# A two-layer attention encoder: its first loads, its x transposes and its bias lines in another order

## The chip, the cores and the metric

The kernel runs on one core of one Trainium2 chip. The metric is the device time of one execution in microseconds (us), as the median of three runs. The profile is one execution taken by the hardware profiler; it has a span (first to last instruction) and a device time of its own.

## The reference, cut to what matters

An input `x` of 512 tokens by 1024 features goes through two layers. Each layer normalises x, projects it with a packed weight matrix, runs four attention branches (A to D) with a gate each, merges them and adds the result to x:

```
for l in range(2):
    h = _rmsnorm(x, norm_gain[l])
    p = _project(h, w_in[l])                       # 1024 -> 13824 columns
    oa = _window_sink_attention(rms(a_q), rms(a_k), a_v, bias_a, sink[l])
    ob = _diff_attention(rms(b_q), rms(b_k), b_v, tbl_b, lam, ...)
    oc = _dense_gqa(rope(c_q), rope(c_k), c_v)
    od = _dilated_attention(rms(d_q), rms(d_k), d_v, bias_d)    # three groups
    for n, o in enumerate((oa, ob, oc, od)):
        y = (o * silu(p['gate'][n])) @ w_branch[l, n]
        merged = merged + sigmoid(p['merge'][n]) * y
    x = x + merged @ w_out[l]
```

`bias_a`, `tbl_b` and `bias_d` come from one small table `rel_bias` (32 buckets by 36 heads), looked up by the distance between query and key. For each head the bias is therefore one line over distances, of which every query sees a shifted piece.

## The kernel before, in words

**Work and tiles.** x is cut into four tiles of 128 tokens (tt = 0 to 3). A tile is normalised (`norm_a`: sum of squares on ACT, scaling on DVE into `h`), transposed, and split into a high and a low f16 part, `hT_h` and `hT_l`, which stay on the chip for the layer. In layer 0, tiles 0 to 2 are transposed on TensorE with the f32 identity (`norm_b`, 8 transposes a tile, then ACT and DVE split them); tile 3 is split first and then transposed by two DMA transposes from SP (`norm_t`, line 247). A projection (`proj_n`, lines 396 to 398) is, for each tile and each of 8 slices of k, three matmuls: high by high, high by low, low by high. For 512 columns that is 24 matmuls a tile.

**Weights.** Weights come in f32 pieces of 1 MB, as two tiles `wst` of 128x1024 each (line 125), with three buffers for such tiles. ACT makes the high part `whi` (line 142), DVE the low part `wlo` (line 143). `take_w` converts three pieces ahead (`AHEAD`) and issues the load of a fourth.

**Bias lines.** `bias_lines` splits `rel_bias` into three f16 parts on DVE (lines 262 to 268), multiplies it with a one-hot table `oh` of 97 rows by 2432 (7 matmuls of 8 output rows, line 274), and writes the result to the first 8 partitions of `acc` (lines 276 and 278). Line 929 then writes these 8 rows 23 times to the DRAM tensor `lines`. `load_bias` (line 542) reads shifted pieces of `lines` as the bias of a head; the first such reader is branch A.

**Order.** The first projections are q of branch A (`proj_q`), then k and v of A (`proj_kv`, 256 columns), then the gate of A beside the attention of A. Each engine runs its instructions in the order in which the program was laid out, so an instruction that waits holds up everything behind it on that engine. This order comes from a scheduler with a timeline of its own; `tc.issue_after(x)` tells it not to place a block ahead of x. SP's queue carries x, the weights, the DMA transposes (`hT`, `qs`, `kk`), `oh`, `lines` and the bias reads; POOL's queue carries the small tables (`gb`, `rope_t`, `sc`, `rbb`, `sk`, `lv`).

**Names in rows.** `mm` is a projection's PSUM tile, `p` that of the bias lines, `s` that of scores, `tr` that of transposes, `pv` that of probabilities by values. `t` is the score with its bias.

Of the kernel before, what the change touches and what calls it, by code (L numbers as in the profile page):

```python
# [11 lines left out]
F32 = mybir.dt.float32  # L12
# [9 lines left out]
HD = 64  # L22
# [65 lines left out]
AHEAD = 3  # L88


@with_exitstack
def encoder(ctx, tc, x, wf, norm_gain, qk_gain, sink, lambda_vec, sub_gain, rel_bias, onehot, rope, out):
# [83 lines left out]
    def load_x(src, tt):  # L176
        if tt % 2 == 0:
            x_sb[tt // 2] = qk.tile([128, 2, D], F32, tag="qx", name="xt", bufs=2)
        nc.sync.dma_start(out=x_sb[tt // 2][:, tt % 2, :], in_=src[tt * 128:tt * 128 + 128, :])
# [23 lines left out]
    with tc.issue_after(dma_w(1).ins):  # L203
        load_x(x, 2)
        nc.sync.dma_start(out=rb, in_=bass.AP(tensor=rel_bias.tensor, offset=rel_bias.offset, ap=[[0, 3], [36, 32], [1, 36]]))
        nc.sync.dma_start(out=oh, in_=onehot)
        load_x(x, 3)

    def norm_a(l, tt):

        xt = x_sb[tt // 2][:, tt % 2, :]
        ss = sm.tile([128, 2], F32, tag="n_ss", name="ss")
        for j in range(2):
            sq = tmp.tile([128, 512], F32, tag="sq", name="sq")
# [5 lines left out]
        S.activation(rs, ln, AF.Exp, scale=-0.5)  # L220
        hs = []
        for j in range(2):
            f = slice(512 * j, 512 * j + 512)
            h = tmp.tile([128, 512], F32, tag="gs", name="h", bufs=4)
            V.scalar_tensor_tensor(h, xt[:, f], rs, gain_b[l][:, f], op0=ALUm, op1=ALUm)
            hs.append(h)
        return hs

    def norm_b(tt, hs):

        for j in range(2):
            tr = transpose4(hs[j])
            d = slice(4 * j, 4 * j + 4)
            c = slice(tt * 128, tt * 128 + 128)
            S.activation(hT_h[:, d, c], tr, AF.Copy, scale=SH)
            done = V.scalar_tensor_tensor(hT_l[:, d, c], tr, SH, hT_h[:, d, c], op0=ALUm, op1=ALUs)
        return done

    def norm_t(tt, hs):

        hi = tmp.tile([128, 2, 512], F16, tag="st", name="h_hi", bufs=3)
        lo = tmp.tile([128, 2, 512], F16, tag="st", name="h_lo", bufs=3)
# [17 lines left out]
    def bias_lines():  # L260
# [7 lines left out]
        V.tensor_tensor(rb16[64:96, :], rb[64:96, :], rb16[64:96, :], op=ALUs)  # L268
        for i, (s0, ln_, h0, nh, off, w) in enumerate(SEG.values()):
            for e in range(0, ln_, 512):  # L270
# [173 lines left out]
    def proj_q(res, l, kind, col, perm=False):  # L444
# [4 lines left out]
        for tt in range(NT):  # L449
# [9 lines left out]
            st = tmp.tile([128, 4, 4, HD], F16, tag="st", name="st", bufs=3)  # L459
# [10 lines left out]
    def proj_k(res, l, kind, col, perm=False):  # L470
# [6 lines left out]
        for tt in range(NT):  # L477
# [33 lines left out]
    def proj_kv(res, l, kind, col):  # L511
# [6 lines left out]
        for tt in range(NT):  # L518
# [7 lines left out]
            st = tmp.tile([128, 4, 128], F16, tag="st", name="st", bufs=3)  # L526
# [59 lines left out]
    def gated(n, ft, gd):  # L586
# [3 lines left out]
        st = tmp.tile([128, 2, 512], F16, tag="st", name="st", bufs=3)  # L590
# [324 lines left out]
    for l in range(L):  # L915
# [109 lines left out]
```

## Time and profile before

| | us |
|---|---|
| median of 3 runs (1674.24 to 1674.72) | 1674.26 |
| device time of the profiled execution | 1674.46 |
| its span | 1672.4 |
| PE busy in it | 1602.6 (96%) |
| DVE busy | 1075.9 (64%) |
| ACT busy | 961.0 (57%) |
| POOL busy | 8.8 (1%) |

PE is busy throughout except at the start: of 40 slices of 41.8 us each, the first shows 3 tenths and the second 3. A busy PE need not be a full one, since matmuls overlap; the granted clock (PEclk) says at which rate it ran. The chain of waits and the waits by engine tell what ended each stretch in which PE stood still. In those two views an engine name with a q (SPq) is the engine's instruction queue, where a DMA is issued.

### The profile page before, as it was taken

The numbers are of one execution on the slowest core, as the hardware profiler recorded it, in microseconds if no ns is written. First come the engines' busy times: TensorE is split into PE (matmuls) and PEld (weight loads), VectorE is DVE, ScalarE is ACT, GpSimd is POOL, SyncE is SP. The second block draws the span as 40 slices with busy tenths as digits, with TensorE's granted clock in tenths as the row PEclk, the third lists the DMA queues.
The fourth block names the chain that finished last, engine by engine and source line by source line (L and its number), as shares of the span: only waits on it lengthen the run. The fifth ranks groups of instructions, "written<-read, shape, count | busy, mean of one in ns | idle before, by whom it ended". The sixth has DMA issues, their size and how long they took to land.

```text
span 1672.4 us, 26438 instructions
## 1 busy us (share of the span) xinstructions
PE 1602.6 (96%) x10302; PEld 834.6 (50%) x10302; DVE 1075.9 (64%) x2104; ACT 961.0 (57%) x1771; POOL 8.8 (1%) x32
## 2 busy tenths in 40 slices
PE   3389999999999999999999999999999999999999
PEld 1155545564555554454445554556455555445444
DVE  3368866785576766575556887678457676657451
ACT  3157676566664656564545767556667464556450
POOL 1000000000000000000000000000000000000000
PEclk8699999999999999999999999999999999999999
DMA  5974733352356757435357483336235674753421
GB/s 188 97 161 133 164 109 95 100 133 76 110 121 155 183 144 191 141 114 143 109 169 173 105 183 119 93 101 133 76 98 130 152 180 132 200 146 94 133 88 51
DMA packets 230817, 218.37 MB, mean 131 GB/s; under 512 B 176316, under 2 KB 188620, under 8 KB 230509
## 3 DMA queue, kind: packets, MB, share of 16 engines
q1 hardware_dynamic: 229925, 214.26, 50.0%
q0 software_dynamic: 768, 2.43, 0.5%
q8 instruction: 80, 1.31, 0.3%
q14 instruction: 44, 0.36, 0.1%
HBM read 163.94 MB, written 10.24 MB: 104 GB/s over the span
## 4 chain that ended last, share of the span: by engine, by line
PE 89%; DMA 6%; DVE 3%; ACT 1%; issue 0%; SPq 0%; DVEq 0%; ACTq 0%
PE mm L396 15%; PE mm L397 15%; PE mm L398 15%; PE mm L407 10%; PE mm L409 10%; PE mm L408 10%; PE s L560 3%; PE s L561 3%; PE pv L565 3%; DMA hT_h<-h_hi 2%; PE pv L567 2%; PE pv L566 2%; DMA oh<-in_onehot_dram 1%; DMA wst<-in_wf_dram 1%; DMA qs<-st 1%; DVE wlo L143 1%
## 5 line engine op out<-in xcount | busy, mean ns | idle before, releaser
L396 PE MATMUL mm<-whi,hT_h 128*128 128x512 f16 (+1 forms) x1408 | 522.7, 371 | 38.7 <-DMA hT_h<-h_hi 31.1
L397 PE MATMUL mm<-wlo,hT_h 128*128 128x512 f16 (+1 forms) x1408 | 522.6, 371 | 0.7 <-DVE wlo L143 0.7
L398 PE MATMUL mm<-whi,hT_l 128*128 128x512 f16 (+1 forms) x1408 | 522.2, 371 | 1.2 <-DMA hT_l<-h_lo 1.2
L143 DVE SCALAR_TENSOR_TENSOR wlo<-wst,whi 128x1024 f16<-128x1024 f32 (+1 forms) x260 | 307.3, 1204 | 203.1 <-ACT whi L142 202.0
L142 ACT ACTIVATE whi<-wst 128x1024 f16<-128x1024 f32 (+1 forms) x260 | 262.6, 1036 | 269.4 <-PE mm L408 122.3
L396 PEld LDWEIGHTS <-hT_h 128*128 128x128 f16 x1408 | 144.4, 103 | 175.9 <-DMA hT_h<-h_hi 32.1
L398 PEld LDWEIGHTS <-hT_l 128*128 128x128 f16 x1408 | 144.4, 103 | 147.6 <-issue 2.6
L397 PEld LDWEIGHTS <-hT_h 128*128 128x128 f16 x1408 | 144.4, 103 | 146.4 <-issue 7.7
L407 PE MATMUL mm<-hT_h,whi 128*128 128x512 f16 x512 | 194.1, 379 | 0.0
L409 PE MATMUL mm<-hT_h,wlo 128*128 128x512 f16 x512 | 194.1, 379 | 0.0
L408 PE MATMUL mm<-hT_l,whi 128*128 128x512 f16 x512 | 194.0, 379 | 0.0
L551 ACT ACTIVATE t<-t,nm 128x512 f32<-128x512 f32 (+2 forms) x224 | 132.0, 599 | 69.1 <-DVE t L811 24.1
L556 DVE TENSOR_TENSOR pl<-t,ph 128x512 f16<-128x512 f32 (+2 forms) x224 | 119.1, 543 | 37.8 <-ACT ph L555 36.5
L565 PE MATMUL pv<-v,ph 128*128 128x65 f16 (+2 forms) x992 | 123.8, 202 | 0.1
L566 PE MATMUL pv<-v,ph 128*128 128x64 f16 (+2 forms) x992 | 122.9, 201 | 0.0
L567 PE MATMUL pv<-v,pl 128*128 128x65 f16 (+2 forms) x992 | 121.0, 199 | 0.0
L409 PEld LDWEIGHTS <-wlo 128*128 128x128 f16 x768 | 75.1, 98 | 88.9
L407 PEld LDWEIGHTS <-whi 128*128 128x128 f16 x768 | 75.1, 98 | 87.1
L408 PEld LDWEIGHTS <-whi 128*128 128x128 f16 x768 | 75.1, 98 | 86.6
L555 ACT ACTIVATE ph<-t 128x512 f16<-128x512 f32 (+2 forms) x224 | 110.9, 506 | 2.8 <-PE pv L567 0.7
L560 PE MATMUL s<-qs,kk 128*128 128x512 f16 (+4 forms) x384 | 99.4, 293 | 1.7 <-DVE gs L582 1.3
L561 PE MATMUL s<-qs,kk 128*128 128x512 f16 (+4 forms) x384 | 100.5, 292 | 0.0
(173 smaller groups left out, 1925.4 us busy)
## 6 DMA issues: line engine op xcount, KB each, us to landing
wst<-in_wf_dram SPq DMA_DIRECT2D x264, 512.0 KB
dsc<-num SPq DMA_DIRECT2D x16, 260.0 KB
xt<-in_x_dram SPq DMA_DIRECT2D x8, 512.0 KB
bias_b<-lines SPq DMA_DIRECT2D x8, 448.0 KB
bias_a<-lines SPq DMA_DIRECT2D x16, 192.0 KB
num<-dsc SPq DMA_DIRECT2D x8, 260.0 KB
n<-dsc SPq DMA_DIRECT2D x8, 260.0 KB
bias_d<-lines SPq DMA_DIRECT2D x32, 64.0 KB
```

The costliest lines, as they stand in the source:

```text
L142: S.activation(hi[:, a], st[:, e:e + step], AF.Copy if sc is SW else AF.Identity, scale=sc)
L143: V.scalar_tensor_tensor(lo[:, a], st[:, e:e + step], sc, hi[:, a], op0=ALUm, op1=ALUs)
L396: PE.matmul(p[:, :ncol], a, wh, start=(k == 0), stop=False)
L397: PE.matmul(p[:, :ncol], a, wl, start=False, stop=False)
L398: PE.matmul(p[:, :ncol], b, wh, start=False, stop=(k == 7))
L407: PE.matmul(p, wh[:, k, f], rh[:, k], start=(k == 0), stop=False)
L408: PE.matmul(p, wh[:, k, f], rl[:, k], start=False, stop=False)
L409: PE.matmul(p, wl[:, k, f], rh[:, k], start=False, stop=(k == nk - 1))
L561: PE.matmul(p, klo, q, start=False, stop=True)
L565: PE.matmul(o, ph, vt[:, 0:d + 1], start=start, stop=False)
L566: PE.matmul(o[:, 0:d], ph, vt[:, d + 2:2 * d + 2], start=False, stop=False)
L567: PE.matmul(o, pl, vt[:, 0:d + 1], start=False, stop=stop)
```

## The change

Six things are altered.

1. Loads. On SP the order of the first loads is x tile 0, gain, weight piece 0, x tile 1, weight piece 1, x tiles 2 and 3, then weights. `rb` and `oh` leave SP for POOL's queue. All tables on POOL now stand behind a one-element copy (`there`) that waits for the last x tile.
2. Weight staging has five buffers (`WST`) instead of three; the conversions of pieces 0 and 1 are placed by `issue_after`.
3. Tile 3 of layer 0 is transposed on TensorE like the others (layer 1 keeps its DMA transposes).
4. `bias_lines` multiplies with `rbr`, in which the 8 heads are repeated 16 times, so that `acc` has the 8 lines on all 128 partitions (16 copies). `lines` is written by two DMAs from POOL, of 128 and of 56 partitions. The call stands behind the k and v projection instead of ahead of it.
5. In `proj_k` the tile `st` of 16x128 is two tiles of 8x128, with a copy and a DMA transpose each; there are four buffers of that tag instead of three.
6. `load_x`, `norm_b` and the block for tables return or use handles for `issue_after`.

```diff
+WST = 5
...
-            st = wp.tile([128, 1024], F32, tag="wst", name="wst", bufs=3)
+            st = wp.tile([128, 1024], F32, tag="wst", name="wst", bufs=WST)
...
     with tc.issue_after(dma_w(1).ins):
         load_x(x, 2)
-        nc.sync.dma_start(out=rb, in_=bass.AP(tensor=rel_bias.tensor, offset=rel_bias.offset, ap=[[0, 3], [36, 32], [1, 36]]))
-        nc.sync.dma_start(out=oh, in_=onehot)
-        load_x(x, 3)
+        last_x = load_x(x, 3)
+
+    there = const.tile([128, 1], F32, name="there")
+    tables = G.tensor_copy(there, x_sb[1][:, 1, 0:1])
...
+        rbr = const.tile([97, len(SEG), 128], F16, name="rbr")
         for i, (s0, ln_, h0, nh, off, w) in enumerate(SEG.values()):
+            V.tensor_copy(rbr[:, i].rearrange("p (c h) -> p c h", h=8),
+                          rb16[:, h0:h0 + 8].unsqueeze(1).to_broadcast([97, 16, 8]))
...
-                PE.matmul(p[:8, :n], rb16[:, h0:h0 + 8], oh[:, c], start=True, stop=True)
+                PE.matmul(p[:, :n], rbr[:, i], oh[:, c], start=True, stop=True)
...
+        for c0, c1_ in ((0, 16), (16, COPIES)):
+            nc.gpsimd.dma_start(out=lines[c0:c1_].rearrange("c h n -> (c h) n"), in_=accf[0:8 * (c1_ - c0), 0:LINE])

     for tt in range(NT):
-        normed = (norm_b if tt < 3 else norm_t)(tt, norm_a(0, tt))
-        if tt < 2:
-            load_w(tt)
+        normed, split = norm_b(tt, norm_a(0, tt))
+        if tt == 0:
+            with tc.issue_after(scaled[0].ins):
+                load_w(0)
+            with tc.issue_after(split.ins):
+                load_w(1)
...
-            st = tmp.tile([128, 16, 128], F16, tag="st", name="st", bufs=3)
-            hi = st[:, 0:8, 0:HD]
+            st = [tmp.tile([128, 8, 128], F16, tag="st", name="st", bufs=4) for _ in range(2)]
+            hi = st[0][:, :, 0:HD]
...
-            V.tensor_copy(st[:, :, HD:128], st[:, :, 0:HD])
-            nc.sync.dma_start_transpose(out=kk[:, :, tt * 128:tt * 128 + 128], in_=st.rearrange("p a d -> p (a d)"))
+            for i in range(2):
+                V.tensor_copy(st[i][:, :, HD:128], st[i][:, :, 0:HD])
+                nc.sync.dma_start_transpose(out=kk[:, 8 * i:8 * i + 8, tt * 128:tt * 128 + 128],
+                                            in_=st[i].rearrange("p a d -> p (a d)"))
...
-            bias_lines()
-            with tc.issue_after(normed.ins):
+            with tc.issue_after(normed.ins), tc.issue_after(tables.ins):
                 gain_tables(0)
+                nc.gpsimd.dma_start(out=rb, in_=bass.AP(tensor=rel_bias.tensor, offset=rel_bias.offset,
+                                                        ap=[[0, 3], [36, 32], [1, 36]]))
+                nc.gpsimd.dma_start(out=oh, in_=onehot)
         run(qa, proj_kv(r, l, "A", 512))
         if l == 0:
-            nc.sync.dma_start(out=lines.rearrange("c h n -> h c n"),
-                              in_=accf[0:8, 0:LINE].unsqueeze(1).to_broadcast([8, COPIES, LINE]))
-            with tc.issue_after(normed.ins):
+            bias_lines()
+            with tc.issue_after(normed.ins), tc.issue_after(tables.ins):
                 setup_columns()
                 setup()
```

**Where the bias matmuls stand on PE.** Before, they follow the first tile's 24 projection matmuls; the transposes of the third tile (L253) stand among them, and the other tiles' projections behind them:

```order
L398 MATMUL mm<-whi,hT_l 128x512
L274 LDWEIGHTS rb_103
L274 MATMUL p<-oh,rb_103 8x512
L274 LDWEIGHTS rb_103
L274 MATMUL p<-oh,rb_103 8x512
L253 MATMUL tr<-ident,h 128x128 x4
L274 LDWEIGHTS rb_103
L274 MATMUL p<-oh,rb_103 8x512
L253 MATMUL tr<-ident,h 128x128 x4
```

Now they follow the last matmul of the k and v projection (L411, 256 columns), and the first scores of branch A (L575, L576) stand among them:

```order
L411 MATMUL mm<-whi,hT_l 128x256
L281 LDWEIGHTS rbr
L281 MATMUL p<-oh,rbr 128x512
L575 LDWEIGHTS kk
L575 MATMUL s<-qs,kk 128x256
L576 LDWEIGHTS kk
L576 MATMUL s<-qs,kk 128x256
L281 LDWEIGHTS rbr
L281 MATMUL p<-oh,rbr 128x512
L575 LDWEIGHTS kk
L575 MATMUL s<-qs,kk 128x384
```

Ahead of the first bias matmul PE now has 32 transposes, 96 projection matmuls of 512 and 96 of 256 columns; before it had 16 and 24 of 512. Behind the last bias matmul come 52 projection matmuls of the gate of A before the fourth block of scores; the first `pv` is PE's row 626 of 20562 in both kernels.

**SP's queue.** Before, with what each instruction waits for (a semaphore of an engine, or DMAHW of an earlier load):

```order
L125 DMA wst<-in_wf_dram 128x1024 [waits DMAHW2_49,DVE_49]
L179 DMA xt<-in_x_dram 128x1024
L205 DMA rb<-in_rel_bias_dram 96x1x36 [waits DMAHW0_49]
L206 DMA oh<-in_onehot_dram 97x2432 [waits DMAHW1_49]
L179 DMA xt<-in_x_dram 128x1024
L125 DMA wst<-in_wf_dram 128x1024 [waits DMAHW3_49,DVE_49]
L125 DMA wst<-in_wf_dram 128x1024 [waits DMAHW5_49,DMAHW4_49,DVE_49]
L125 DMA wst<-in_wf_dram 128x1024 [waits DMAHW6_49,DVE_49]
L929 DMA lines<-acc 8x23x2432 [waits DVE_49,Activation_49]
```

Now, the same place, from the second half of weight piece 1 on:

```order
L126 DMA wst<-in_wf_dram 128x1024 x2
L180 DMA xt<-in_x_dram 128x1024
L180 DMA xt<-in_x_dram 128x1024 [waits DMAHW0_49]
L126 DMA wst<-in_wf_dram 128x1024 [waits DMAHW1_49]
L126 DMA wst<-in_wf_dram 128x1024 [waits DMAHW2_49,DVE_49]
L126 DMA wst<-in_wf_dram 128x1024 [waits DMAHW3_49,DVE_49]
L126 DMA wst<-in_wf_dram 128x1024 [waits DMAHW5_49,DMAHW4_49,DVE_49]
```

The second `wst` of piece 1 no longer waits for a buffer (DVE), x tiles 2 and 3 follow at once, and `oh` and `lines` are gone from this queue.

**DVE after the first tile's projection.** Now the conversions of pieces 2 and 3 (L144) stand ahead of the last two tiles' halves `hT_l` (L240):

```order
L431 TENSOR_REDUCE ss<-sq 128x8
L144 SCALAR_TENSOR_TENSOR wlo<-wst,whi 128x1024
L229 SCALAR_TENSOR_TENSOR h<-xt,rs,gain_b 128x512 x2
L144 SCALAR_TENSOR_TENSOR wlo<-wst,whi 128x1024
L229 SCALAR_TENSOR_TENSOR h<-xt,rs,gain_b 128x512 x2
L144 SCALAR_TENSOR_TENSOR wlo<-wst,whi 128x1024
L471 TENSOR_TENSOR qn<-mm,rs 128x512
L144 SCALAR_TENSOR_TENSOR wlo<-wst,whi 128x1024
L431 TENSOR_REDUCE ss<-sq 128x8
L240 SCALAR_TENSOR_TENSOR hT_l<-tr,hT_h 128x4x128 x2
L266 TENSOR_SCALAR rb<-rb 96x36
```

Before, the bias table's first rows (L262 on) stood here, and three conversions in a row followed the third tile.

## Rows read from the trace of the kernel before

**Rows 1.** Page, part 1: busy us of each engine (share of the span) and instructions.

```profile
PE 1602.6 (96%) x10302; PEld 834.6 (50%) x10302; DVE 1075.9 (64%) x2104; ACT 961.0 (57%) x1771; POOL 8.8 (1%) x32
```

**Rows 2.** Busy time by stretch: length, engines with counts, PEclk, DMA share, GB/s.

```profile
0.00:22.60 22.60, 11.38 (x40) 5.06 (x40) 10.96 (x21) 12.71 (x29) 4.67 (x18) 1.00 0.76 250
22.60:38.00 15.40, 0.16 (x1) 0.08 (x1) 2.30 (x7) 0.50 (x2) 0.00 (x0) 0.64 0.38 137
38.00:56.40 18.40, 16.76 (x62) 6.81 (x61) 13.98 (x28) 10.14 (x24) 0.54 (x1) 0.74 0.45 78
56.40:86.50 30.10, 0.00 (x0) 0.00 (x0) 3.47 (x5) 1.54 (x2) 0.53 (x1) 0.58 1.11 111
86.50:114.60 28.10, 26.09 (x156) 16.40 (x157) 19.35 (x60) 13.60 (x40) 0.00 (x0) 0.90 0.90 186
114.60:131.60 17.00, 15.74 (x78) 7.37 (x77) 10.80 (x22) 13.88 (x27) 0.00 (x0) 1.00 0.34 78
131.60:1672.40 1540.80, 1532.44 (x9969) 798.85 (x9967) 1015.08 (x1966) 908.61 (x1647) 3.08 (x12) 1.00 0.49 129
```

**Rows 3.** Waits of PE, 0 to 132: who for whom, total, times, longest.

```profile
PE mm L396 <- DMA hT_h<-h_hi: 30.2, 1, 30.2
PE p L274 <- DMA oh<-in_onehot_dram: 15.3, 1, 15.3
```

**Rows 4.** The chain that ended last, in order of time: start, length, what.

```profile
13.82 24.16 DMA oh<-in_onehot_dram
...
56.13 30.37 DMA hT_h<-h_hi
...
340.42 2.54 DMA bias_d<-lines
```

**Rows 5.** SP's queue in order of time: start, length, instruction.

```profile
44.25 0.31 SPq L929 DMA_DIRECT2D lines<-acc  x1
...
56.13 25.60 SPq L247 DMA_TRANSPOSE hT_h<-h_hi  x1
...
104.96 6.97 SPq L531 DMA_TRANSPOSE kk<-st  x3
```

**Rows 6.** DMA queues, 30 to 38 us: packets, MB, share of 16 engines.

```profile
q1 hardware_dynamic: 44, 0.21, 6.2%
```

**Rows 7.** The same, 64 to 80 us.

```profile
q1 hardware_dynamic: 81, 0.79, 44.9%
```

**Rows 8.** The same, 544.9 to 545.8 us (a store of 128 rows of 2080 bytes).

```profile
q1 hardware_dynamic: 113, 0.20, 58.4%
```

**Rows 9.** DMA issues: count, KB each, us to landing (750 to 765; then 0 to 140).

```profile
gb<-in_qk_gain_dram POOLq DMA_DIRECT2D x1, 256.0 KB, 4.7
...
lines<-acc SPq DMA_DIRECT2D x1, 1748.0 KB
...
oh<-in_onehot_dram SPq DMA_DIRECT2D x1, 460.8 KB
```

**Rows 10.** DVE groups, 0 to 114.65: line, shape, count, busy, mean ns, idle before.

```profile
L143 DVE SCALAR_TENSOR_TENSOR wlo<-wst,whi 128x1024 f16<-128x1024 f32 x10 | 12.0, 1216 | 30.2 <-ACT whi L142 30.2
...
L530 DVE COPY st<-st 128x256 f16<-128x256 f16 x4 | 0.9, 219 | 0.0
```

**Rows 11.** Instructions in order of time: start, length, engine, line.

```profile
5.93 0.16 DVE L216 TENSOR_TENSOR ss<-ss 128x1 f32<-128x1 f32 x1 [5.93 <-ACT sq L215]
...
10.00 1.15 ACT L142 ACTIVATE whi<-wst 128x512 f16<-128x512 f32 x2 [3.29 <-DMA wst<-in_wf_dram]
...
117.42 0.38 PE L397 MATMUL mm<-wlo,hT_h 128*128 128x512 f16 x1
117.64 0.38 PE L398 MATMUL mm<-whi,hT_l 128*128 128x512 f16 x1
...
131.60 0.19 PE L565 MATMUL pv<-v,ph 128*128 128x65 f16 x1
```

**Rows 12.** Waits of PE, 120 to 1672.

```profile
PE mm L396 <- DVE v L496: 2.3, 2, 1.6
```

More of the change, by code (lines that the diff above doesn't have):

```diff
@@ L178, in load_x @@
             x_sb[tt // 2] = qk.tile([128, 2, D], F32, tag="qx", name="xt", bufs=2)
-        nc.sync.dma_start(out=x_sb[tt // 2][:, tt % 2, :], in_=src[tt * 128:tt * 128 + 128, :])
+        return nc.sync.dma_start(out=x_sb[tt // 2][:, tt % 2, :], in_=src[tt * 128:tt * 128 + 128, :])
     gain_b = {}
@@ L204, in encoder @@
         load_x(x, 2)
-        nc.sync.dma_start(out=rb, in_=bass.AP(tensor=rel_bias.tensor, offset=rel_bias.offset, ap=[[0, 3], [36, 32], [1, 36]]))
-        nc.sync.dma_start(out=oh, in_=onehot)
-        load_x(x, 3)
+        last_x = load_x(x, 3)
+    there = const.tile([128, 1], F32, name="there")
+    tables = G.tensor_copy(there, x_sb[1][:, 1, 0:1])
+    scaled = [None]
     def norm_a(l, tt):
@@ L219, in norm_a @@
         rs = sm.tile([128, 1], F32, tag="n_rs", name="rs")
-        S.activation(rs, ln, AF.Exp, scale=-0.5)
+        scaled[0] = S.activation(rs, ln, AF.Exp, scale=-0.5)
         hs = []
@@ L234, in norm_b @@
             c = slice(tt * 128, tt * 128 + 128)
-            S.activation(hT_h[:, d, c], tr, AF.Copy, scale=SH)
+            split = S.activation(hT_h[:, d, c], tr, AF.Copy, scale=SH)
             done = V.scalar_tensor_tensor(hT_l[:, d, c], tr, SH, hT_h[:, d, c], op0=ALUm, op1=ALUs)
-        return done
+        return done, split
     def norm_t(tt, hs):
-        hi = tmp.tile([128, 2, 512], F16, tag="st", name="h_hi", bufs=3)
-        lo = tmp.tile([128, 2, 512], F16, tag="st", name="h_lo", bufs=3)
+        hi = tmp.tile([128, 2, 512], F16, tag="st", name="h_hi", bufs=4)
+        lo = tmp.tile([128, 2, 512], F16, tag="st", name="h_lo", bufs=4)
         for j in range(2):
@@ L273, in bias_lines @@
                 p = ps_mm.tile([128, 512], F32, tag="mm", name="p")
-                PE.matmul(p[:8, :n], rb16[:, h0:h0 + 8], oh[:, c], start=True, stop=True)
+                PE.matmul(p[:, :n], rbr[:, i], oh[:, c], start=True, stop=True)
                 if i % 2:
-                    S.activation(accf[0:8, c], p[:8, :n], AF.Copy, scale=1.0 / SB)
+                    S.activation(accf[:, c], p[:, :n], AF.Copy, scale=1.0 / SB)
                 else:
-                    V.tensor_scalar(accf[0:8, c], p[:8, :n], 1.0 / SB, None, op0=ALUm)
+                    V.tensor_scalar(accf[:, c], p[:, :n], 1.0 / SB, None, op0=ALUm)
+        for c0, c1_ in ((0, 16), (16, COPIES)):
+            nc.gpsimd.dma_start(out=lines[c0:c1_].rearrange("c h n -> (c h) n"), in_=accf[0:8 * (c1_ - c0), 0:LINE])
     for tt in range(NT):
-        normed = (norm_b if tt < 3 else norm_t)(tt, norm_a(0, tt))
-        if tt < 2:
-            load_w(tt)
+        normed, split = norm_b(tt, norm_a(0, tt))
[4 more added lines that the diff above has]
+                load_w(1)
     maxb = const.tile([128, 36], F32, name="maxb")
@@ L458, in proj_q @@
             V.tensor_tensor(heads(qn), heads(src), rs.unsqueeze(2).to_broadcast([128, 8, HD]), op=ALUm)
-            st = tmp.tile([128, 4, 4, HD], F16, tag="st", name="st", bufs=3)
+            st = tmp.tile([128, 4, 4, HD], F16, tag="st", name="st", bufs=4)
             qv = qn.rearrange("p (a b d) -> p a b d", a=4, b=2)
@@ L481, in proj_k @@
             V.tensor_tensor(heads(kg), heads(p), tabs[l][:, n:n + 1, :].to_broadcast([128, 8, HD]), op=ALUm)
-            st = tmp.tile([128, 16, 128], F16, tag="st", name="st", bufs=3)
-            hi = st[:, 0:8, 0:HD]
+            st = [tmp.tile([128, 8, 128], F16, tag="st", name="st", bufs=4) for _ in range(2)]
+            hi = st[0][:, :, 0:HD]
             S.activation(hi, heads(kg), AF.Copy, scale=KS)
-            V.scalar_tensor_tensor(st[:, 8:16, 0:HD], heads(kg), KS, hi, op0=ALUm, op1=ALUs)
-            V.tensor_copy(st[:, :, HD:128], st[:, :, 0:HD])
-            nc.sync.dma_start_transpose(out=kk[:, :, tt * 128:tt * 128 + 128], in_=st.rearrange("p a d -> p (a d)"))
+            V.scalar_tensor_tensor(st[1][:, :, 0:HD], heads(kg), KS, hi, op0=ALUm, op1=ALUs)
+            for i in range(2):
+                V.tensor_copy(st[i][:, :, HD:128], st[i][:, :, 0:HD])
+                nc.sync.dma_start_transpose(out=kk[:, 8 * i:8 * i + 8, tt * 128:tt * 128 + 128],
+                                            in_=st[i].rearrange("p a d -> p (a d)"))
             yield
@@ L525, in proj_kv @@
                 V.tensor_tensor(heads(kg), heads(p[:, 0:128]), tabs[l][:, 0:1, :].to_broadcast([128, 2, HD]), op=ALUm)
-            st = tmp.tile([128, 4, 128], F16, tag="st", name="st", bufs=3)
+            st = tmp.tile([128, 4, 128], F16, tag="st", name="st", bufs=4)
             hi, lo = st[:, 0:2, 0:HD], st[:, 2:4, 0:HD]
@@ L589, in gated @@
             gT[n] = big.tile([128, 4, 2, T], F16, tag="gT", name="gT", bufs=2)
-        st = tmp.tile([128, 2, 512], F16, tag="st", name="st", bufs=3)
+        st = tmp.tile([128, 2, 512], F16, tag="st", name="st", bufs=4)
         gf = gd.rearrange("p a b -> p (a b)")
```

## The prediction, made before the changed kernel was run

> **What bounds the kernel now.** I read the page's first part for the limiting engine, then busy time by stretch for where it is not at work, then its waits and the chain for why. PE is busy for 1602.6 us of 1672.4 [rows 1]. From the first `pv` at 131.6 [rows 11] to the end it is busy for 1532.4 of 1540.8 us at full clock [rows 2], and its largest group of waits in that part makes 2.3 us [rows 12]. So nothing behind 131.6 us can give back more than 1540.8 - 1532.4 = 8.4 us, and the question is only how early the first `pv` comes. Up to there PE is busy for 11.38 + 0.16 + 16.76 + 0 + 26.09 + 15.74 = 70.1 us, of which the stretches from 38.0 and from 86.5 ran at a mean clock of 0.74 and 0.90 [rows 2]. The reader is to see two holes of 15.4 and 30.1 us [rows 2], and who ends them: the one-hot table `oh` (15.3 us) and the DMA transpose of x's fourth tile (30.2 us) [rows 3]; the chain names the same two [rows 4].
>
> The first hole: `oh` is issued at 13.8 and is the chain's step for 24.2 us [rows 4]. From 30 to 38 us the DMA engines move 0.21 MB with 6.2% of 16 engines [rows 6], which is 1.0 engine at 26 GB/s; 460.8 KB [rows 9] at that rate are 18 us. Its 97 rows ride on one engine, and whatever SP issues later has a share queued behind it there. The second hole: `lines` is issued at 44.25, and the transpose behind it sits on SP from 56.13 for 25.6 us [rows 5]. From 64 to 80 us SP's queue moves 81 packets with 44.9% of 16 engines for 16 us [rows 7], 1.42 us a packet. `lines` has 184 rows of 9728 bytes, 1.79 MB in all (1748 KB [rows 9]).
>
> **The change part by part.**
>
> *Both waits go.* PE's bias matmuls now stand behind 192 projection matmuls, so `oh` has until PE is through with k and v; the fourth tile needs no DMA transpose, so it no longer stands behind `lines`. What is late next is worked out here from DVE, since it is the engine with the most to do at the start.
>
> *DVE.* Between 0 and 114.6 us, just ahead of the first bias addition, DVE was busy for 10.96 + 2.30 + 13.98 + 3.47 + 19.35 = 50.1 us [rows 2], for the same list as it now has: 10 conversions of 1.2 us [rows 10], the norms, the tables, q, k and v. (The fourth tile's two splits only change their source.) New are five copies into `rbr`; the nearest row, 0.219 us [rows 10], makes 1.1 us. That is 51.2 us. It starts at 5.9 [rows 11]. In the first 22.6 us it was idle for 22.6 - 5.9 - 11.0 = 5.7 us, waiting for loads, while six small tables on POOL shared the DMA engines. With these behind x, the first weight, which ACT got at 10.0 [rows 11], should come 1.8 us earlier (estimate: x's first tile, the gain and that weight are 1.57 MB, 6.3 us at the 250 GB/s of [rows 2], and some 1.9 us go for issue and landing: 8.2), so I take 3.9. The bias matmuls are interleaved with scores that need the `kk` transposes, three of which took 6.97 us on SP [rows 5]; I give DVE 3 us of waiting there. Last eviction of the bias lines: 5.9 + 51.2 + 3.9 + 3 = 64 us.
>
> *PE up to there.* Its own list is 96 matmuls of 0.22 us (117.42 to 117.64 [rows 11]), 96 of half the columns, and 32 transposes (counted at 0.16, an estimate): 37 us, and with a start at 10 and 24 matmuls at half clock some 52. DVE needs until 57 for k and v (64 less the 7 us in which three `kk` transposes go out [rows 5]). So PE waits for DVE for at least 5 us, and the order shows where: at the third tile's `hT_l`, behind the conversions of pieces 2 and 3, and at a PSUM tile of k, behind pieces 4 and 5 and the last q eviction; I expect 3 to 5 us at each. Its bias matmuls end with DVE, at 64. Then 52 gate matmuls of 0.22 last to 75.4.
>
> *Lines and the first bias.* The fourth block of scores needs a PSUM tile freed by the first bias addition. Lines leave at 64. A store from 128 partitions moves 0.20 MB with 58.4% of 16 engines in 0.9 us [rows 8]: 24 GB/s an engine. Eight rows an engine and then four are 12 x 9728 / 24 = 4.9 us. A POOL load of 0.26 MB landed 4.7 us after its issue [rows 9], 0.7 of it data by the same rate, so 4.0 us go for issue and landing: 8.9 us. A read of `lines` then cost the chain 2.5 us [rows 4]. First bias addition: 64 + 8.9 + 2.5 = 75.4, level with PE. Bounds: at the least the 4.7 us of that load; at the most the old 1.42 us a packet, 12 x 1.42 + 4.0 = 21 us. I take 8.9, since the source rows now lie on all partitions as in [rows 8].
>
> *From there to the first `pv`.* 44 gate matmuls (9.7 us) and ten short score matmuls (some 1.4): 86.5, say 87, against 131.6. ACT and DVE need about 8 us for the four blocks in that time, which PE's work hides.
>
> *Costed at nothing.* POOL's tables wait for the last x, at 19 us or sooner (4.7 MB at 250 GB/s [rows 2]); their 1.5 MB take 6 us at that rate, and 4 us more as above make 29, while DVE has some 23 us of work ahead of the first of them and so wants it at about 32. `oh`: even on one engine it lands at 20 + 18 = 38, or at 56 if weights take half of that engine, against 57 at PE; the cover is 19 us or, at worst, 1. Eight more transposes on PE (some 1.3 us) lie in its waits for DVE. Five weight buffers only let SP issue earlier. In all layers, `proj_k` gets 32 more DVE copies and 32 more DMA transposes; the largest group of PE's waits after 120 us is for a DVE split, not for `kk` [rows 12], and these lie beside PE's other work.
>
> *Clock.* PE was at 1.2 GHz for part of the stretches after each hole: 26% of speed lost over 18.4 us (4.8 us), 10% over 28.1 (2.8 us) [rows 2]. These costs are in the 131.6. The two waits of 4 us left are between what kept the clock and what lost it; I add 1.5 us.
>
> *Sum.* Span 87 + 1540.8 + 1.5 = 1629.3; the profiled run took 1674.46 for a span of 1672.4, so 2.1 more: 1631.4. Its median stands 0.2 below it: 1631 us, 43 us faster.
>
> **The rivals.**
>
> *Lines stay slow.* If a 9728-byte row costs 1.42 us whatever partition it comes from, lines take 21 us, the first bias comes at 87.5, and PE stands for 12 us at its fourth block of scores: 1643. For it: that is the only rate of such packets here [rows 7]. Against: other stores from 128 partitions run at 24 GB/s an engine [rows 8]. The Trainium skill, "DMA: Bandwidth & Descriptors" (section on why a DMA increments its semaphore by 16), says that a DMA gets the largest number of engines up to 16 that divides its outermost sizes; that is 8 engines for 8 rows before, 16 and 14 now, and it speaks of the number of engines alone, so by that rule taken alone this rival holds. Chance 0.17.
>
> *PE is the limit from the start.* If loads come so early that DVE never holds PE, the first `pv` comes after the first transposes' start at about 7.7 and 70.1 us of PE work less the 7.6 lost to clock, with some 4 us of waits: 74 to 76, 12 us earlier: 1619. Against: DVE's 51 us must fit behind 5.9 in order. Chance 0.13.
>
> *The clock falls in both waits, or `kk` lands late behind weights on SP.* 4.8 + 2.8 us in place of 1.5: 1637. The Trainium skill, "TensorE: Matmul & The Clock Gate" (Part 1), says that an idle PE returns to 1.2 GHz; the trace agrees for waits of 15 and 30 us [rows 2], and no row shows one of 4 us. Chance 0.14.
>
> *Slower.* Each tile of k now needs two DMA transposes on SP behind two copies, ahead of weights and bias reads. If the second half makes PE wait at each of the 32 tiles, 43 / 32 = 1.35 us each would eat the gain, and beyond that the kernel is slower: 1680 at 1.5 us. Against: 8.4 us idle in all behind 131.6 [rows 2]. Chance 0.04.
>
> **How the numbers follow.** The forecast (1625 to 1637) has 0.5, the four rivals 0.48, and 0.02 is left for what I don't see. The range of 1619 to 1645 takes in the early and the late rival. A change under 0.2% (3.3 us, what a measurement of this kernel can tell from none) would need the whole start to stay as long: 0.01. Faster 0.95, slower 0.04.
>
> **What would show it.** Right: no wait of PE for `oh` or `hT_h<-h_hi` before 100 us; the first `pv` at 84 to 91; waits of some 4 us for DVE `hT_l` and `qn`; the first bias addition at 73 to 78; 1540 us behind the first `pv`. Wrong: a wait of 10 us or more at scores for DVE `t` (slow lines), a first `pv` before 80 (DVE was not the limit), or more than 1545 us behind it.

## The result, and the profile after

The changed kernel took 1636.41 us (median of 4 runs, 1634.80 to 1638.10) against 1674.25 for the kernel before in the same session: a ratio of 0.9773 [0.9757, 0.979], 38 us faster, where 1631 us was forecast. The profiled run took 1634.8 us for a span of 1632.7: 2.1 us lie outside the span, as before.

The page's first part for the changed kernel, busy us of each engine, answering to [rows 1]:

```profile
PE 1601.6 (98%) x10310; PEld 835.6 (51%) x10310; DVE 1074.1 (66%) x2141; ACT 957.7 (59%) x1771; POOL 12.2 (1%) x37
```

PE works 1.0 us less than before; the other 39 us of span are time in which it stood. Busy time by stretch, with the columns of [rows 2]; the third of these stretches ends at the first `pv`:

```profile
25.70:49.50 23.80, 17.65 (x100) 10.36 (x100) 23.31 (x58) 10.39 (x25) 0.97 (x2) 0.93 0.77 218
49.50:62.80 13.30, 11.06 (x67) 7.12 (x67) 9.97 (x40) 7.44 (x26) 0.04 (x1) 0.87 0.62 169
62.80:88.30 25.50, 22.70 (x101) 10.11 (x99) 9.95 (x20) 13.84 (x27) 1.04 (x2) 0.93 0.44 140
88.30:1632.70 1544.40, 1533.63 (x9969) 799.47 (x9967) 1014.10 (x1998) 905.86 (x1648) 3.10 (x12) 1.00 0.48 128
```

The two empty stretches of [rows 2] are gone: PE is busy in every stretch (16.55 us in the first 25.7), and DVE is now the fullest engine between 25.7 and 49.5 (23.31 of 23.80 us). Behind the first `pv` the kernel needs 1544.40 us, against 1540.80. There PE idles for 1544.40 - 1533.63 = 10.8 us, before for 8.4, and is busy for 1.2 us more: the loss of 3.6 us.

The four largest groups of PE's waits up to 100 us (who for whom: total, times, longest), answering to [rows 3]:

```profile
PE tr L257 <- DVE h L229: 8.6, 2, 7.6
PE mm L409 <- DVE qn L471: 4.4, 2, 3.2
PE s L575 <- DVE t L668: 2.7, 1, 2.7
PE tr L257 <- DVE hT_l L240: 1.7, 1, 1.7
```

PE waits neither for `oh` nor for the DMA transpose `hT_h<-h_hi` any more; but for the start (7.6 us), the longest wait is 3.2. The same behind the first `pv`, answering to [rows 12]:

```profile
PE mm L411 <- DMA hT_l<-h_lo: 4.7, 1, 4.7
PE mm L409 <- DVE qn L471: 1.2, 1, 1.2
```

The first line is one wait of 4.7 us for a DMA transpose at the boundary of the two layers. Before, PE stood there for 1.2 us:

```profile
PE mm L398 <- DMA hT_l<-h_lo: 1.2, 1, 1.2
```

The chain between 55 and 92 us, in order of time (start, length, what), answering to [rows 4]:

```profile
62.77 0.53 POOL lines L288
63.30 7.70 DMA lines<-acc
71.14 3.71 DMA bias_a<-lines
```

Here the start ends: POOL issues `lines` behind the last eviction, 8.4 us later the first bias read goes out, and it takes 3.7 us. DVE's rows show how long it had been idle by then (the bracket is the idle time before, and who ended it):

```profile
61.78 0.42 DVE L285 TENSOR_SCALAR acc<-p 128x256 f32<-128x256 f32 x1
...
74.88 1.53 DVE L668 SCALAR_TENSOR_TENSOR t<-s,rsk,bias_a 128x256 f32<-128x256 f32 x3 [12.55 <-DMA bias_a<-lines]
```

Its last eviction of the bias lines starts at 61.78; one short copy later it stands for 12.55 us until the bias arrives. The other transfer that made a hole before, `oh`, was issued on POOL at 19.04 and landed 7.9 us later (the last number), where before it took 24.16 us [rows 4]:

```profile
oh<-in_onehot_dram POOLq DMA_DIRECT2D x1, 460.8 KB, 7.9
```

In the trace its 97 packets lie between 22.3 and 26.0 us, before between 17.9 and 37.6. POOL's queue (q0) from 22.5 to 26.5 us (packets, MB, share of 16 engines):

```profile
q0 software_dynamic: 317, 0.83, 85.6%
```

`oh` and the small tables beside it, 0.83 MB in all, went by that queue with 85.6% of 16 engines, where [rows 6] shows one engine at work.

### The profile page after: what moved, and what is told of

Read it like the earlier page. It is cut to its first block, busy times and chain, and to the rows that moved or that the text cites. A ratio compares the mean times of both kernels' runs of the same rounds, so it can differ in the third digit from the quotient of the medians.

```text
span 1632.7 us, 26578 instructions
## 1 busy us (share of the span) xinstructions
PE 1601.6 (98%) x10310; PEld 835.6 (51%) x10310; DVE 1074.1 (66%) x2141; ACT 957.7 (59%) x1771; POOL 12.2 (1%) x37
## 4 chain that ended last, share of the span: by engine, by line
PE 92%; DVE 2%; DMA 2%; issue 1%; ACT 1%; POOL 0%; SPq 0%; ACTq 0%
PE mm L411 16%; PE mm L409 16%; PE mm L410 16%; PE mm L420 10%; PE mm L421 10%; PE mm L422 10%; PE s L575 3%; PE s L576 3%; PE pv L580 3%; PE pv L581 2%; PE pv L582 2%; DVE wlo L144 1%; DMA hT_l<-h_lo 1%; DMA lines<-acc 0%; DMA qs<-st 0%
## 5 line engine op out<-in xcount | busy, mean ns | idle before, releaser
L411 PE MATMUL mm<-whi,hT_l 128*128 128x512 f16 (+1 forms) x1408 | 522.7, 372 | 4.7 <-DMA hT_l<-h_lo 4.7
L144 DVE SCALAR_TENSOR_TENSOR wlo<-wst,whi 128x1024 f16<-128x1024 f32 (+1 forms) x260 | 304.6, 1202 | 128.6 <-ACT whi L143 127.8
L143 ACT ACTIVATE whi<-wst 128x1024 f16<-128x1024 f32 (+1 forms) x260 | 256.8, 1034 | 147.2 <-PE mm L421 123.3
L411 PEld LDWEIGHTS <-hT_l 128*128 128x128 f16 x1408 | 144.6, 103 | 151.5 <-DMA hT_l<-h_lo 5.2
L429 ACT ACTIVATE sq<-mm 128x512 f32<-128x512 f32 (+1 forms) x96 | 51.8, 539 | 89.4 <-PE mm L411 88.3
L575 PE MATMUL s<-qs,kk 128*128 128x512 f16 (+4 forms) x384 | 99.4, 293 | 3.8 <-DVE t L668 2.7
```

The lines of the kernel that those rows point to most:

```text
L143: S.activation(hi[:, a], st[:, e:e + step], AF.Copy if sc is SW else AF.Identity, scale=sc)
L144: V.scalar_tensor_tensor(lo[:, a], st[:, e:e + step], sc, hi[:, a], op0=ALUm, op1=ALUs)
L411: PE.matmul(p[:, :ncol], b, wh, start=False, stop=(k == 7))
L575: PE.matmul(p, khi, q, start=True, stop=False)
```

## The experiments

All kernels here compute the whole reference. A ratio is to the kernel before in runs of the same session, with its 95% interval in brackets; where there is none, the kernel ran once, and its time stands alone.

**Where the 3.6 us behind the first `pv` went: three buffers, or the old `st` tile.**

```diff
-WST = 5
+WST = 3
```

> The changed kernel with three weight buffers (WST = 3) as before; all else of the change stays. Two theories for the 3.6 us that the stretch behind the first pv lost (1540.8 to 1544.4 us), which I put down to PE's new 4.7 us wait for hT_l<-h_lo at 838 us. Theory A: with five buffers both halves of a weight piece are ready together, so DVE takes both conversions ahead of the h_lo splits of layer 1's fourth tile, and the DMA transpose of it goes out late. Then three buffers put the splits back between the two conversions: the wait at 838 us falls from 4.7 to under 2 us, the clock does not fall there, the stretch behind the first pv is 1540 to 1541.5, and the whole is 2 to 4 us less than the changed kernel unless the start, whose weights come later, gives some back (first pv 88 to 91). Theory B: the wait comes from the k projection's two smaller st tiles with four buffers and their extra transposes: then it stays at 4 to 5 us, the stretch at 1544, the whole at 1636.

Measured: 1631.09 us, 0.9749 [0.9735, 0.9762]. First `pv` at 88.4, and from there:

```profile
88.40:1628.20 1539.80, 1532.35 (x9969) 799.15 (x9967) 1018.17 (x2003) 912.04 (x1653) 3.10 (x12) 1.00 0.49 130
```

1539.8 us, the whole loss back and 1 us more. These are the numbers of theory A; whether its cause holds too is taken up below. The waits behind the first `pv`:

```profile
PE mm L409 <- DMA hT_h<-h_hi: 1.2, 1, 1.2
PE mm L411 <- DMA hT_l<-h_lo: 1.0, 1, 1.0
```

The start did not get worse, though SP's second half of weight piece 1 and so x's last tiles went out later.

```diff
-WST = 5
+WST = 4
-            st = [tmp.tile([128, 8, 128], F16, tag="st", name="st", bufs=4) for _ in range(2)]
+            st = tmp.tile([128, 16, 128], F16, tag="st", name="st", bufs=3)
...
```

> The changed kernel with the k projection's st in one 16x128 tile, three buffers and one DMA transpose a tile as before; weight buffers are four, since five don't fit beside it. Theory A (conversions of a piece stand together ahead of h_lo): the wait for hT_l<-h_lo at 838 us stays at 4 to 5 us and the stretch behind the first pv at 1543 to 1545; the whole within 2 us of 1636. Theory B (the split st tiles make it): the wait is under 2 us, the stretch 1541, the whole 1632 to 1634. On the split itself: if the 32 more transposes and copies cost anything steady, this is faster by more than the wait explains; I expect not.

Measured: 1631.81 us, 0.9759 [0.9742, 0.9776]; first `pv` at 85.7, 1543.4 us behind it, and

```profile
PE mm L411 <- DMA hT_l<-h_lo: 4.9, 1, 4.9
```

The wait stays without the split: theory B falls. The whole is faster mainly for another reason, an earlier start by 2.6 us. Buffers and `st` tile were changed together there, so which of them brings it is open.

**What exactly waits at the boundary.**

```diff
-            norm_t(3, last)
+            norm_b(3, last)
```

> The changed kernel with layer 1's fourth tile also transposed on TensorE (norm_b in place of norm_t). If the lost time behind the first pv is that one wait and the fall of the clock behind it: 4.7 us of wait and 3.4 us (6.8 us at 1.2 GHz) go, eight transposes (some 1.3 us) and a short wait for their splits come: the stretch behind the first pv is 1537.5 to 1541 in place of 1544.4, the whole 1629 to 1633. If the time is lost elsewhere, spread over the layers, the stretch stays at 1543 or more though the wait is gone.

Measured: 1633.71 us, 0.9762 [0.9749, 0.9775]; 1543.2 us behind the first `pv`. I had expected the wait to vanish, and it did not:

```profile
842.89 0.61 PE L411 MATMUL mm<-whi,hT_l 128*128 128x512 f16 x1 [3.81 <-DMA hT_l<-h_lo]
```

So I had named the wrong tile: PE waits for the third tile's `hT_l`, not the fourth's. SP's queue shows why (start, length, instruction), first of the changed kernel, then with three buffers:

```profile
830.70 1.67 SPq L251 DMA_TRANSPOSE hT_h<-h_hi  x1
832.47 1.14 SPq L126 DMA_DIRECT2D wst<-in_wf_dram  x2
833.78 1.42 SPq L251 DMA_TRANSPOSE hT_l<-h_lo  x1
```

```profile
830.84 1.90 SPq L251 DMA_TRANSPOSE hT_h<-h_hi  x1
832.84 1.15 SPq L126 DMA_DIRECT2D wst<-in_wf_dram  x1
834.09 1.63 SPq L251 DMA_TRANSPOSE hT_l<-h_lo  x1
835.82 0.51 SPq L126 DMA_DIRECT2D wst<-in_wf_dram  x1
```

The transpose of `hT_l` goes out at the same time, 833.8 and 834.1, but two weight loads of 512 KB stand ahead of it in the one and one load in the other; PE's wait for it ends at 842.95 and at 839.14. With three buffers the second load stands behind the transpose. DVE's order, my theory A, is not needed for it. To test the queue, the next kernel keeps five buffers and queues weight loads behind any transposes that stand ahead of them in the program:

```diff
-            dma = nc.sync.dma_start(out=st, in_=src[:, e:e + 1024])
+            with (tc.issue_after(hold[0].ins) if hold else nullcontext()):
+                dma = nc.sync.dma_start(out=st, in_=src[:, e:e + 1024])
...
-            nc.sync.dma_start_transpose(out=t[:, :, tt * 128:tt * 128 + 128], ...)
+            dma = nc.sync.dma_start_transpose(out=t[:, :, tt * 128:tt * 128 + 128], ...)
+        hold[:] = [dma]
```

> The changed kernel, with one order added: at the boundary of the layers no weight load is issued on SP ahead of the DMA transposes of layer 1's tiles that stand before it in the program. The runs with three buffers, and with the fourth tile on TensorE, showed that PE's wait at 838 us is for the third tile's hT_l, whose transpose was issued at the same time in both (833.8 and 834.1 us) but landed 3.7 us later where two weight loads of 512 KB stood between hT_h and hT_l on SP and not one. If the queue is the cause: the wait goes to under 1.5 us with five buffers too, the stretch behind the first pv is 1539 to 1541 us, the whole 3 to 5 us less than the changed kernel, 1631 to 1633. If the order of DVE (conversions ahead of the h_lo splits) is the cause instead: the wait stays above 3 us. A cost on the other side: four loads then land together behind the transposes, and a piece that k and v need could come late (a wait for whi or wlo).

Measured: 1637.3 us, 0.9793 [0.978, 0.9807]: no gain. The wait moved by one tile:

```profile
830.25 1.24 SPq L253 DMA_TRANSPOSE hT_l<-h_lo  x1
831.54 2.00 SPq L128 DMA_DIRECT2D wst<-in_wf_dram  x4
...
837.03 6.51 SPq L253 DMA_TRANSPOSE hT_h<-h_hi  x1
```

```profile
845.65 0.45 PE L412 MATMUL mm<-whi,hT_h 128*128 128x512 f16 x1 [5.21 <-DMA hT_h<-h_hi]
```

PE no longer waits for the third tile's `hT_l`, but the four loads now go out together at 831.5, ahead of the fourth tile, whose `hT_h` sits on SP for 6.5 us and holds PE for 5.2. The total was missed, since loads held back stand ahead of the next transpose.

All runs together say more than this one. In each of the ten kernels here with four or five buffers PE waits at this place, for 3.8 to 6.7 us, for a transpose with two or more weight loads right ahead of it on SP. In the four with three buffers (the kernel before, the one above and two below) there is one load, and PE's longest wait for these transposes is 1.1 to 1.4 us. So the number of buffers brings the wait. That it does so through the order on SP's queue is what the rows speak for; the run made to show it only moved the wait.

**Is DVE the pace of the start?** The set-up work (maxima of the biases, sinks, lambda) moves behind the last eviction of the bias lines, and the tables that it loads go to tiles of the probabilities:

```diff
-            with tc.issue_after(normed.ins), tc.issue_after(tables.ins):
+            with tc.issue_after(evicted.ins), tc.issue_after(tables.ins):
                 setup_columns()
                 setup()
...
-            rbb = at.tile([128, 16, 36], F32, tag="bias", name="rbb")
+            rbb = at.tile([128, 16, 36], F32, tag=("ph", "pl")[i], name="rbb")
...
-        gb = at.tile([128, L * 8, HD], F32, tag="bias", name="gb")
+        gb = at.tile([128, L * 8, HD], F32, tag="ph", name="gb")
```

> The changed kernel, with the 7 us of small DVE work of the set-up (maxima of the biases, gains, sinks) queued behind the last eviction of the bias lines; its loads go to tiles of the probabilities, so that they need not wait. Theory A (DVE sets the pace of the start, 19.5 us busy of 20 between 20 and 40 us): the waits for qn (4.4 us in two) and for t (2.7 us) shrink, the last eviction comes at 56 to 58 in place of 62, the first bias addition at 69 to 72 in place of 74.9, the first pv at 83 to 86 in place of 88.3; the whole 2 to 5 us less. Rival: PE then waits for what comes next (kk transposes, whi of later pieces) and the first pv stays at 87 to 89.

Measured: 1626.69 us, 0.9724 [0.9711, 0.9738], the lowest median here; its interval lies below that of the changed kernel. First `pv` at 80.1, even earlier than theory A said. Its stretches up to there, from 25.7 us on:

```profile
25.70:49.50 23.80, 20.78 (x126) 12.76 (x126) 21.64 (x54) 12.35 (x33) 0.54 (x1) 0.93 0.84 245
49.50:62.80 13.30, 11.04 (x63) 5.72 (x62) 11.36 (x37) 5.31 (x16) 1.08 (x2) 1.00 1.01 261
62.80:80.10 17.30, 16.37 (x79) 7.58 (x78) 8.97 (x24) 11.59 (x24) 0.00 (x0) 1.00 0.25 78
```

and DVE's rows:

```profile
56.96 0.42 DVE L285 TENSOR_SCALAR acc<-p 128x256 f32<-128x256 f32 x1
...
57.42 2.24 DVE L326 TENSOR_REDUCE maxb<-rbb 128x36 f32<-128x576 f32 x2
...
69.69 1.53 DVE L669 SCALAR_TENSOR_TENSOR t<-s,rsk,bias_a 128x256 f32<-128x256 f32 x3 [3.12 <-DMA bias_a<-lines]
```

Between 25.7 and 49.5 PE works 20.78 us in place of 17.65. The last eviction comes at 57.0 (61.8), the first bias addition at 69.7 (74.9), with the set-up in the gap. That is 5 us; the other 3 lie behind the first bias addition, where PE needs 10.4 us to the first `pv` in place of 13.4. Its waits for `qn` at 49.5 and for `t` are gone or under 1 us, and with them the falls of the clock (1.00 in place of 0.87 and 0.93). The boundary is not touched by it: 1544.7 us behind the first `pv`, with a wait of 6.7 us for `hT_l`.

**The latency from the last eviction to the bias, hidden behind k.** On top of the fourth tile's `norm_b`:

```diff
-        run(qa, proj_kv(r, l, "A", 512))
+        run(qa)
+        if l == 0:
+            bias_lines()
+        run(proj_kv(r, l, "A", 512))
```

> As t3pe, and in layer 0 the bias matmuls and the stores of lines stand ahead of the projection of k and v, not behind. Theory A: the 12.6 us from the last eviction of the bias lines to the first bias addition are latency (store, issue, read) that now lies beside the projection of k; PE's wait of 2.7 us for t and the fall of the clock behind it (1.7 us) go, and DVE's idle 12.5 us fill: first pv at 80 to 85, the whole 4 to 8 us under t3pe, 1622 to 1628. Rival: DVE sets the pace, so that what is put ahead of k only pushes k back by the same time (four or five evictions, some 3 us), and k's transposes then come last: first pv at 87 to 89, the whole level with t3pe.

Measured: 1635.89 us, 0.9775 [0.9761, 0.9789]; first `pv` at 91.5. The first bias addition comes 10 us earlier, at 64.7, but the rival holds, and more:

```profile
PE s L575 <- DMA kk<-st: 4.8, 2, 3.2
PE p L281 <- DVE acc L285: 3.2, 1, 3.2
```

PE waits for the evictions, and then for the `kk` transposes, 3.2 us for one of them; those were hidden while the bias came last.

**The gains together.** First the edits of the runs with the old `st` tile, with held loads and with deferred set-up in one:

> Three in one: the old st tile of the k projection with four weight buffers (first pv at 85.7 us), no weight loads ahead of the boundary's transposes, and the set-up work behind the bias lines. If they add: first pv 82 to 84, 1539 to 1541 behind it, with 2.1 outside the span 1624 to 1627, against 1636 for the changed kernel. If the first pv is held by the DMA of kk or by the loads: 85.7 as it was, 1627 to 1629.

Measured: 1629.56 us, 0.9742 [0.9728, 0.9756]; first `pv` at 82.6 and 1545.8 us behind it, since the held loads hold PE at the boundary here too. The start was within the forecast, the boundary was not. Then deferred set-up with three buffers, and x's last tiles free to go ahead:

```diff
-WST = 5
+WST = 3
...
-    with tc.issue_after(dma_w(1).ins):
-        load_x(x, 2)
-        last_x = load_x(x, 3)
+    dma_w(1)
+    load_x(x, 2)
+    last_x = load_x(x, 3)
```

> Changed kernel with the set-up work behind the bias lines (that alone: first pv 80.1, stretch behind it 1544.7, 1626.7 us), three weight buffers (alone: stretch behind the first pv 1539.8), and x's last two tiles issued ahead of the second half of weight piece 1, which three buffers make wait. If the two gains add: first pv 79 to 84, 1539 to 1541 behind it, whole 1620 to 1626. If the later weights hold the start (five buffers let SP load further ahead): first pv 84 to 88, whole 1626 to 1630.

Measured: 1628.54 us, 0.9728 [0.9713, 0.9742]. 1539.6 us behind the first `pv`, as with three buffers alone, but the first `pv` only at 86.2: the second theory. PE waits once for 4.9 us at the third tile. ACT shows why (the bracket as above):

```profile
28.52 1.06 ACT L143 ACTIVATE whi<-wst 128x1024 f16<-128x1024 f32 x1 [3.96 <-DMA wst<-in_wf_dram]
...
29.96 1.08 ACT L239 ACTIVATE hT_h<-tr 128x512 f16<-128x512 f32 x2
```

It stands in order for a weight that three buffers let come later, and the third tile's `hT_h` is behind it. The gains do not add; this kernel and the one with deferred set-up can't be told apart by their intervals.

**Why `lines` is quick.** The same transfer from eight partitions, side by side and 17 apart:

```diff
-        for c0, c1_ in ((0, 16), (16, COPIES)):
-            nc.gpsimd.dma_start(out=lines[c0:c1_].rearrange("c h n -> (c h) n"), in_=accf[0:8 * (c1_ - c0), 0:LINE])
+        nc.gpsimd.dma_start(out=lines.rearrange("c h n -> h c n"),
+                            in_=accf[0:8, 0:LINE].unsqueeze(1).to_broadcast([8, COPIES, LINE]))
```

> The changed kernel, but lines is written from the first eight partitions alone, each read 23 times, as before (on POOL's queue as now). Packets of 9728 bytes took 1.42 to 1.49 us each before the change and 0.37 after it. Theory A (the source: many engines read the same few partitions): 1.4 us a packet or more again, lines take some 27 to 34 us from 63 us on, the first bias addition at 95 to 102, first pv at 104 to 112, whole 1652 to 1662. Theory B (SP's queue made it slow, POOL's is fast): 0.4 us a packet, lines as quick as in the changed kernel apart from the number of engines (8 in place of 16: 23 rows each x 0.4 = 9 us), first bias at 78.

(the second kernel reads `accf[0:120:17, 0:LINE]`)

> The changed kernel, but lines is written from eight partitions, each read 23 times, and these eight lie 17 apart (0, 17, ..., 119) in place of side by side (0 to 7), which gave 37.5 us for lines and a first pv at 116.9. Theory A (neighbouring partitions share a way out of SBUF): spread over the array the packets are quick again, 0.4 to 0.7 us, 23 a source make 9 to 16 us, the first bias addition at 77 to 86, first pv at 90 to 98. Theory B (the number of engines or of source partitions alone, eight in both): as with 0 to 7, 1.4 us or more a packet, first bias at 100 to 105.

Measured: 1663.59 and 1645.57 us. The chain's step of each, first side by side:

```profile
61.19 37.47 DMA lines<-acc
```

```profile
63.01 20.05 DMA lines<-acc
```

The step takes 37.5, 20.1 and, from 128 partitions, 7.7 us. POOL's queue during it (packets, MB, share of 16 engines), side by side from 62 to 100 us, spread from 63.5 to 83.5, and of the changed kernel from 63 to 71.5:

```profile
q0 software_dynamic: 384, 1.79, 38.1%
```

```profile
q0 software_dynamic: 384, 1.79, 45.6%
```

```profile
q0 software_dynamic: 224, 1.79, 58.3%
```

Each moved the 184 rows of 9728 bytes. At 16 engines' time by the shares, 38 x 16 x 0.381 / 184 makes 1.26 us a row side by side, 0.79 spread and 0.43 from 128 partitions (the small packets counted in). So POOL's queue is not enough to make `lines` quick, and the place of the eight sources alone is worth 17 us (one run each). The last 12 us go with 128 sources, where the number of source partitions and that of engines change together. The packets of the traces give each a share: a row takes 0.76 us at the median from eight partitions 17 apart and 0.37 from 128, and at most 10 rows are under way at a time in the first case and 20 in the second. Why a row is quicker from 128 partitions, no run here shows. By the rule on the number of engines of the Trainium skill ("DMA: Bandwidth & Descriptors", why a DMA increments its semaphore by 16) an engine has 23 rows from eight sources and 8 + 4 = 12 from 128. By that alone the estimate is 37.5 x 12 / 23 = 19.6 us; the trace's 7.7 agrees only together with the place of the sources.

**`oh` on SP again.**

```diff
+        nc.sync.dma_start(out=rb, in_=bass.AP(tensor=rel_bias.tensor, ...))
+        nc.sync.dma_start(out=oh, in_=onehot)
         last_x = load_x(x, 3)
...
-                nc.gpsimd.dma_start(out=oh, in_=onehot)
```

> The changed kernel with rel_bias and the one-hot table oh loaded on SP between x's third and fourth tile, as before. In the changed kernel oh comes on POOL behind x and its 97 rows land within 4 us. Theory A (the queue spreads the rows): on SP they ride on one engine for 18 to 24 us again, so x's fourth tile and the first weights have a share queued behind it: the fourth tile and pieces 2 and 3 come late, PE waits 5 to 15 us more between 20 and 45 us, first pv at 93 to 103, whole 1641 to 1651. Theory B (now that the bias matmuls stand behind k, oh's slowness hides): first pv at 88 to 90, the whole within 3 us of the changed kernel.

Measured: 1652.25 us, 0.987 [0.9853, 0.9886], above the interval of the changed kernel. First `pv` at 105.8, beyond theory A's range. The chain:

```profile
8.49 28.36 DMA xt<-in_x_dram
```

x's fourth tile takes 28.4 us from its issue, with part of it queued behind `oh` on one engine (24 GB/s from 30 us on), and PE stands for it:

```profile
43.34 1.09 PE L259 MATMUL tr<-ident,h 128*128 128x128 f32 x4 [19.34 <-DVE h L231]
```

**One part of the change on the kernel before: the fourth tile on TensorE.**

```diff
-        normed = (norm_b if tt < 3 else norm_t)(tt, norm_a(0, tt))
+        normed = norm_b(tt, norm_a(0, tt))
```

> The kernel before, with one part of the change alone: x's fourth tile transposed on TensorE like the others. The 30 us wait for hT_h goes. Theory A: lines, slow and on SP as before, then hold PE in the same place of time: it waits for the first bias addition, at about 86 us, and what is gained is only the gate matmuls that no longer stand behind that wait: first pv at 100 to 118, whole 1642 to 1660. Theory B: the hole was the DMA transpose's alone and all of it comes back: first pv at 101 or less, 1642 at the most.

Measured: 1674.35 us in its one run, no gain; first `pv` at 133.2. Both theories fall. PE's longest wait and the chain:

```profile
PE mm L396 <- ACT hT_h L235: 27.9, 2, 25.9
```

```profile
46.37 35.94 DMA wst<-in_wf_dram
82.33 1.06 ACT whi L142
...
83.93 0.61 PE mm L396
```

Without the DMA transpose the next thing that SP issues behind `lines` is late in its place: weights issued at 46.4 land at 82.3. ACT stands in order at their conversion (27.0 us), with the fourth tile's `hT_h` behind it, and so PE waits 25.9 us for a tile that it had transposed at 55.7. The second hole was that of everything behind `lines` on SP.

## Why the prediction was right

*Both holes go.* Right, in place and size. The first `pv` came at 88.3, against 86.5 to 87 and 1.5 us for the clock. But what ends a hole is not the whole of its cause. Taken back one at a time, the many sources of `lines` cost some 28 us (first `pv` at 116.9 against 88.3, in one run) and `oh`'s place 16 us (1652.25), while the fourth tile's transposes on TensorE, which take away the wait that ends the second hole in [rows 3], bring nothing alone on the kernel before.

*DVE's pace.* Right: 51.2 us of work were counted and 16.79 + 23.31 + 9.97 = 50.1 seen up to 62.8; the last eviction was forecast at 64 and seen at 61.8 to 62.2. With some 7 us of DVE's work moved behind that eviction the start ended 8.2 us earlier.

*PE's two waits of 3 to 5 us.* Right in place, smaller in size: 1.7 us at `hT_l` and 3.2 at `qn`.

*Lines and the first bias.* Right: 8.9 and 2.5 us forecast, 8.4 and 3.7 seen, first addition forecast at 75.4, seen at 74.88. The forecast had PE level with it there; PE was 2.7 us early and stood for `t`. The rival of slow lines was wrong: a row does not cost the same whatever partition it comes from (0.37 us at the median here, where the forecast's 24 GB/s make 0.41 and the rival took 1.42).

*`oh` costed at nothing.* Right for POOL's queue, but the working, "even on one engine", was too mild: on SP ahead of x's fourth tile it costs 16 us, by what queues behind it and not by its own landing.

*The clock.* 1.5 us was the right size, in part by luck. It was set down for the two waits at `hT_l` and `qn`. The clock did fall at both, as the third rival had it (0.77 from 29.4 to 36.0 us, 0.51 from 49.5 to 52.9), but there DVE set the pace (23.31 us busy of 23.80 between 25.7 and 49.5, 3.16 of 3.44 behind that), so that little of it need show in the time; that is argued, no run parts it. It fell once more behind the wait for `t`, which the prediction did not have, and this lies on the way to the first `pv` (PEclk is the third last number):

```profile
75.70:80.50 4.80, 4.65 (x16) 1.87 (x15) 4.35 (x10) 4.72 (x11) 0.00 (x0) 0.64 0.18 67
```

36% of 4.8 us is 1.7 us.

*The failed step: "Five weight buffers only let SP issue earlier", costed at nothing, and with it "unchanged at 1540.8" behind the first `pv`.* Issuing earlier has a cost: at the boundary of the layers two loads get ahead of a transpose that PE needs next. It measured 3.6 us, 1544.4 against 1540.8, and three buffers give 1539.8. That the buffers cost it is shown; that they do so through SP's queue rests on the rows of that queue. The split `st` tiles do not make this wait. The median lies 5.4 us above the forecast: these 3.6, less 0.2 at the start (88.3 for 88.5), 1.6 between the profiled run (1634.8) and the median (1636.41), and 0.4 between the 1631.4 forecast for the profiled run and the 1631 for the median.

## What to carry to other kernels

Ask of a hole not only what ended it but what else stood behind the same transfer: take away the one waiter, and the next in that queue can be late by nearly as much (here PE waited 25.9 us in place of 30.2). Where many short jobs share one engine at the start, move those that nobody needs yet into the gap behind its last needed result: that was worth 8 us more here (ratios of 0.9724 and 0.9773). More buffers for a load are a change of order on its queue; look at which transfers it now overtakes.

## What the runs showed of the hardware that was not expected

- The time of `lines` by its source: 37.5 us from eight neighbouring partitions, 20.1 from eight that lie 17 apart, 7.7 from 128 (the last with more engines too).
- The same 97 rows of `oh` moved in 19.7 us on SP's queue, from 30 us on with one engine at work, and in 3.7 us on POOL's, while that queue held 85.6% of 16 engines.
- At waits of PE of 2.7, 3.2 and 4.7 us the granted clock fell for a few us. Around the 4.7 us wait of the changed kernel at the boundary (length, engines, and PEclk as the third last number):

```profile
842.90:850.00 7.10, 7.05 (x21) 2.72 (x22) 0.76 (x2) 0.72 (x2) 0.00 (x0) 0.62 0.59 125
850.00:860.00 10.00, 10.00 (x69) 6.49 (x67) 6.19 (x8) 6.50 (x12) 0.00 (x0) 1.00 0.29 77
```

0.62 is a mean of the two levels of 1.2 and 2.4 GHz over the 7.1 us behind the wait; 10 us on it is 1.00. In the kernel with deferred set-up, where after 49.5 us no wait of PE before the first `pv` exceeds 1.8 us, it is 1.00 throughout those stretches. The length of a single wait does not settle it: in both kernels the clock also fell at 29 to 30 us, at the last of three waits of 0.9 to 1.7 us (0.77 from 29.4 to 36.0 in the changed kernel). The trace agrees with the Trainium skill, "TensorE: Matmul & The Clock Gate" (Part 1), that a TensorE that stands returns to 1.2 GHz, now for waits shorter than the 15 and 30 us of [rows 2].
